# Adding each expert's rows to the tokens' rows in DRAM by accumulating indirect DMAs

## The chip, the core and the metric

The kernel runs on one core of a Trainium2 chip. The metric is device time in microseconds (us), the median of several executions. A profiled execution is taken beside them; its trace is what this text reads. The engines are named as the trace names them: PE is TensorE (matmul), PEld its weight loads, DVE is VectorE, ACT is ScalarE, POOL is GpSimd, SP is SyncE, which here only issues DMAs. A q behind a name (SPq) is that engine's instruction sequencer.

## What is computed

Two blocks run one after the other on 512 tokens of 1024 numbers. The first (`first_block`: recurrent and sparse attention layers) isn't touched by the change. The second has two layers; each mixes tokens (attention, convolution, memory) and then sends every token through two of 16 experts:

```python
def grouped_moe(x2d, w_router, router_bias, w_gate, w_up, w_down):
    logits = (x2d @ w_router).astype(jnp.float32) + router_bias.astype(jnp.float32)
    scores = jax.nn.softmax(logits, axis=-1)
    grouped = scores.reshape(T, N_GROUPS, EXPERTS_PER_GROUP)
    g_idx = jnp.argmax(jnp.max(grouped, axis=-1), axis=-1)
    in_group = jnp.take_along_axis(grouped, g_idx[:, None, None], axis=1)[:, 0]
    top_vals, top_idx = lax.top_k(in_group, TOP_K)
    experts = g_idx[:, None] * EXPERTS_PER_GROUP + top_idx
    weights = top_vals / jnp.sum(top_vals, axis=-1, keepdims=True)
    ...
        h = jax.nn.silu(xblk @ w_gate[e]) * (xblk @ w_up[e])
        return h @ w_down[e]
    ...
    return jax.ops.segment_sum(y, buf_tok, num_segments=T + 1)[:T]
```

The layer's end is `x = layer_norm(DEEPNORM_ALPHA * x + f, ln2_g[l], ln2_b[l])` with `f` from the function above. Gate and up weights of an expert are 1024 by 512, the down weights 512 by 1024, all fp32: 2 MB each, 6.29 million bytes an expert. With 512 tokens and two choices each there are 1024 rows for 16 experts, 64 on average. With these inputs every expert of the first layer has between 43 and 90 tokens; in the second layer they have between 22 and 142, and expert 15 alone has more than 128.

## The kernel before

Each matmul of an fp32 activation with an fp32 weight is done as three matmuls of rounded parts (high by high, high by low, low by high; `mm3`, L183 to L185). A weight tile (512 KB) is loaded on SP's queue by `wload` (L1622, tiles `wr` and `mr`, up to nine of them in buffers), and `wsplit` makes its high part on ScalarE (L1636) and its low part on VectorE (L1637).

`moe` (L1758) runs one layer's experts in order. Each expert has 128 slots, filled from slot 0 by the rank of a token among those that chose the expert. The rows of experts 0 and 1 are picked by matmuls with one-hot matrices (`expert_in`). For experts 2 to 14, `slot_tokens` (L1683) works out on VectorE and TensorE which token sits in which slot (`idx`, L1712; a free slot gets an index past the last token), and `expert_fetch` (L1715) gathers the tokens' rows from the DRAM copy `x1d` by an indirect DMA on POOL (L1718), three experts ahead; `expert_turn` transposes them on TensorE (L1729). `expert_up` does gate and up, `expert_down` (L1749) the down product of the expert before. Its two halves are copied out of PSUM by ScalarE (L1755, tile `yo`) and written to the expert's 128 slots in DRAM, `yd`, by two DMAs of 256 KB on ScalarE's queue (L1756).

Before expert 2, a loop (L1769 to L1783) runs once for every block of 128 rows by which experts overflow their slots: not at all in the first layer, once in the second. It loads that expert's weights again, and writes its rows to further slots of `yd`. So that slots never written hold numbers, `clear_slots` (L1481) writes 8 blocks of zeros (512 KB each) to `yd` early in the kernel, some 1400 us before they are used.

`x1d` holds the layer's normalised tokens. `after_mix` (L1398) and `late_copy` (L1433) write it, with `put` (L538): two SP DMAs of 256 KB for each of four tiles of 128 tokens.

At a layer's end `weigh` (L1592) gives each token's two weights (done beside expert 2), and the four token tiles are loaded back from `x1d` in eight SP DMAs of 256 KB, issued in program order at expert 14. Expert 15 keeps its rows on chip. The rows of experts 0 to 14 come back from `yd` by eight indirect gathers on POOL (`yg`, L1829, 512 KB each: four token tiles, two choices), and are added with their weights on VectorE (`add`, L1838; ten instructions a layer) and, for some, by fp32 matmuls with diagonal matrices on TensorE (L1846; `dg` made on POOL, L1821). Expert 15's rows are added by matmuls with its one-hot matrix (L1848, `ct`) and an addition from PSUM (L1849). `combine(0, ..)` makes tiles 0 and 1 ready, whose layer norm follows (L1313 to L1327); `combine(2, ..)` does tiles 2 and 3 and is ordered behind the statistics of the first two (`stats_end`). The work on the tail is ordered by hand: `issue_after` keeps an instruction behind a named one.

A tile's `tag` and `bufs` set how many buffers it shares; the scheduler places waits where a buffer, a PSUM bank or a DRAM tensor is written again or read after a write.

Of the kernel before, what the change touches and what calls it, by code (L numbers as in the profile page):

```python
# [33 lines left out]
ON_PE = [(2, 0), (3, 0)]  # L34
RAW = 5, 2
ORDER = (0, 2, 1, 2, 0, 2, 2, 1, 2, 0, 2, 1)
SLOTS = (16 + N_OV) * P
# [3 lines left out]
T2 = (26, 29, 45, 21)  # L41
# [6 lines left out]
class K:  # L48
# [515 lines left out]
    def hawk(self, x, after, prep, masks, rest):  # L564
# [833 lines left out]
    def after_mix(self, l, xs, i0, gb, pl, sc, x1):  # L1398
# [27 lines left out]
        if late:  # L1426
            self.parted = self.split_end[0]
        else:
            for a in range(2):
                self.affine(xs[a], xs[a], gb, nc.gpsimd, nc.gpsimd)  # L1430
                self.put(self.x1d[l], a, xs[a])

    def late_copy(self, l, xs, gb):  # L1433

        for i in range(2, 4):
            with self.tc.issue_after(self.routed.ins):
                self.affine(xs[i], xs[i], gb, self.nc.vector, self.nc.gpsimd)
            self.put(self.x1d[l], i, xs[i])

    def moe_constants(self):  # L1440
# [37 lines left out]
        self.yd = self.dp.tile([SLOTS, D], F32, name="yd")  # L1478
        self.x1d = [self.dp.tile([T, D], F32, name=f"x1d{l}") for l in range(2)]

    def clear_slots(self):  # L1481

        nc = self.nc
        z = self.rt("zero")
        nc.gpsimd.memset(z, 0.0)
        blocks = [self.yd[i * P:(i + 1) * P] for i in range(15, 16 + N_OV)]
        self.later += [lambda d=d: nc.sync.dma_start(d.rearrange("p (h c) -> p h c", h=2),
                                                      z[:, None, :].to_broadcast([P, 2, 512])) for d in blocks]
# [103 lines left out]
    def weigh(self, oh1, oh2, sc, slotf):  # L1592
# [10 lines left out]
        wl, w1 = [self.small([4], name=f"rwl{j}", bufs=1) for j in range(2)]  # L1603
        tt(wl, oh1[:, :, 15], wv[:, 0], op=OP.mult)
        tt(w1, oh2[:, :, 15], wv[:, 1], op=OP.mult)
        tt(wl, wl, w1, op=OP.add)
        slot = self.small([4, 2], I32, name="rslot", bufs=1)
        nc.vector.tensor_copy(slot.rearrange("p i j -> p j i"), slotf)
        return slot, wv, wl
# [73 lines left out]
    def slot_tokens(self, ohs, rank):  # L1683
# [4 lines left out]

        tok = self.small([2, 4, 16], name="tok", bufs=1)
        for u in range(2):  # L1690
            nc.gpsimd.iota(tok[:, u], pattern=[[u * P, 4], [0, 16]], base=0, channel_multiplier=1 - u,
                           allow_small_or_imprecise_dtypes=True)
# [3 lines left out]
        tk = self.small([2, 4, 2, 16], BF16, name="stk", bufs=1)  # L1696
        at = self.ph.tile([P, 2, 4, P], BF16, name="at", tag="t2", bufs=self.bufs["t2"])
        for j, oh in enumerate(ohs):
            tt(a, oh, rank, op=OP.mult)
            nc.vector.tensor_reduce(r[:, j], a, axis=AX.X, op=OP.add)  # L1700
            for u in range(2):
                tt(tk[:, j, :, u], oh, tok[:, u], op=OP.mult)
            for i in range(4):
                nc.vector.tensor_scalar(at[:, j, i], self.iota, r[:, j, i:i + 1], None, op0=OP.is_equal)
        for j in range(2):
            for i in range(4):
                nc.tensor.matmul(ps[:, :32], at[:, j, i], tk[:, j, i].rearrange("p u e -> p (u e)"),
                                 start=j == 0 and i == 0, stop=j == 1 and i == 3)
        idx = self.small([16], I32, name="idx", bufs=1)
        hi = self.small([16], name="idh", bufs=1)  # L1710
        nc.vector.tensor_copy(hi, ps[:, 16:32])
        tt(idx, ps[:, :16], hi, op=OP.add)  # L1712
        return idx
# [35 lines left out]
    def expert_down(self, hT, wd, yrow, own=False):  # L1749
        nc = self.nc  # L1750
        for c in range(2):
            py = self.pj()
            self.tm(self.wrows(wd[:, c * 512:(c + 1) * 512], 4, own), hT, py)
            yo = self.t2(F32, "yo")
            nc.scalar.copy(yo, py)  # L1755
            nc.scalar.dma_start(yrow[:, c * 512:(c + 1) * 512], yo)  # L1756

    def moe(self, l, xs, rt):  # L1758
# [10 lines left out]
        def overflow():  # L1769
            nov = nc.values_load(ovi[0:1, 7:8], min_val=0, max_val=N_OV)  # L1770
            with tc.For_i(0, nov, 1) as b:
                ev = nc.values_load(ovi[0:1, bass.ds(b, 1)], engines=[mybir.EngineType.SP], min_val=0, max_val=15)
                row = b * P + 16 * P
                we = [w[bass.ds(ev, 1)].rearrange("o k c -> (o k) c") for w in W]
                oh = self.f4(F32R, "oh").rearrange("p (i a s) -> p i a s", i=4, a=2)
                for i in range(4):
                    nc.vector.tensor_scalar(oh[:, i, 1], cur, slotf[:, 0, i:i + 1], None, op0=OP.is_equal)
                    nc.vector.scalar_tensor_tensor(oh[:, i, 0], cur, slotf[:, 1, i:i + 1], oh[:, i, 1].bitcast(F32),
                                                   op0=OP.is_equal, op1=OP.add)
# [3 lines left out]
                self.expert_down(hT, we[2], self.yd[bass.ds(row, P)], True)  # L1783

        xT = [[[v[:, a * P:(a + 1) * P] for v in t] for t in xT] for xT in [self.expert_in(l, xs, oh, 256)] for a in range(2)]
        idx = self.slot_tokens((oh1, oh2), rank)
        fetched = {e: self.expert_fetch(l, idx, e) for e in (2, 3)}
        hT = None
        for e in range(16):
# [8 lines left out]
            if e == 15:  # L1798
                self.expert_down(hT, W[2][14], self.yd[14 * P:15 * P])
            h2 = self.expert_up(xT[e], *[self.wrows(W[j][e], 8, first=first.pop(0) if first else None) for j in range(2)])  # L1800
            if e == 2:
                slot, wv, wl = self.weigh(oh1, oh2, sc, slotf)
            if e == 14:
                f = [self.load_x(self.x1d[l], i) for i in range(4)]
            if 0 < e < 15:
                self.expert_down(hT, W[2][e - 1], self.yd[(e - 1) * P:e * P])
# [7 lines left out]
        pw = self.pt()  # L1814
        for i in range(4):
            nc.tensor.matmul(pw[:, :1], oh[:, i].bitcast(F32), wl[:, i:i + 1], start=i == 0, stop=i == 3)
        dg = self.t2(F32, "dg")
        for i in range(2):
            for j in range(2):
                k = 2 * i + j  # L1820
                nc.gpsimd.tensor_scalar(dg[:, k * P:(k + 1) * P], self.ident, wv[:, j, i + 2:i + 3], None, op0=OP.mult)  # L1821
        ws = self.small([1], name="ws", bufs=1)
        nc.vector.tensor_copy(ws, pw[:, :1])
        raws = [self.wload(W[2][15][:, c * 512:(c + 1) * 512], 4) for c in range(2)]
        gs = []
        for i in range(4):
            for j in range(2):
                g = self.eh.tile([P, D], F32, name="yg", tag="mr", bufs=RAW[0]) if j else self.f4(F32, "yg")
                nc.gpsimd.indirect_dma_start(out=g, out_offset=None, in_=self.yd,  # L1829
                                             in_offset=bass.IndirectOffsetOnAxis(ap=slot[:, i, j:j + 1], axis=0))  # L1830
                gs.append(g)
        half = [slice(h * 512, (h + 1) * 512) for h in range(2)]

        def add(i, j):
            for h in range(2):
                if (i, h) in ON_PE:
                    continue
                nc.vector.scalar_tensor_tensor(f[i][h], gs[2 * i + j][:, half[h]], wv[:, j, i:i + 1], f[i][h],  # L1838
                                               op0=OP.mult, op1=OP.add)

        def combine(p, h):
            for i in range(p, p + 2):
                ps = self.pj()
                for j in range(2) if (i, h) in ON_PE else (1,) if p else ():
                    k = 2 * i + j - 4
                    nc.tensor.matmul(ps, dg[:, k * P:(k + 1) * P], gs[2 * i + j][:, half[h]], start=j == 0 or (i, h) not in ON_PE, stop=False)  # L1846
                for part in range(2):
                    nc.tensor.matmul(ps, ct[:, i * P:(i + 1) * P], y[h][part], start=not p and part == 0, stop=part == 1)  # L1848
# [3 lines left out]
        mark = self.split_end[0]  # L1852
        for c in range(2):
            py = self.pj()
            ws2 = list(self.wsplit(raws[c]))
            if c:
                with tc.issue_after(mark.ins):
                    for i in range(2):
                        for j in range(2):
                            add(i, j)  # L1860
            for k, wk in enumerate(ws2):
# [4 lines left out]
            last = nc.scalar.activation(h, py, AF.Identity, bias=0.0, scale=ws)  # L1866
            self.lo(lo, py, h, ws)
# [4 lines left out]
        for i in range(2, 4):  # L1872
            with tc.issue_after(mark.ins):
                add(i, 0)
        with tc.issue_after(self.stats_end.ins):
            for h in range(2):
                combine(2, h)
# [26 lines left out]
def body(tc, I, out, stop=None):  # L1904
    with ExitStack() as es:
# [55 lines left out]
        if stop and stop.endswith("1"):  # L1961
            src = I["hawk_out"][0]
            with k.phase("pre", t2=34, e=(2,), r=8):
# [6 lines left out]
                if stop == "first1":  # L1970
                    k.clear_slots()
# [76 lines left out]
```

## Time and profile before

| | before |
|---|---|
| median of 3 runs | 2987.15 us (2984.01 to 2990.06) |
| profiled execution | 2984.6 us, span of the trace 2982.8 us |
| granted TensorE clock over the span | 0.979 of full |
| experts, first layer | about 1615 to 1950 us |
| experts, second layer | about 2595 to 2960 us |

The span runs from the first to the last recorded instruction. The chain of waits goes back from the last instruction, at each step to what released it. In the timeline a row is an instruction or a run of equal ones: start, duration, engine and line, what is written from what, and in brackets how long the engine was idle before it and what it waited for. Durations of matmuls overlap, since they are pipelined. The windows show each engine's busy time in a stretch, the granted clock of TensorE (1.00 is full speed), the mean busy share of 16 DMA engines, and the rate at which they moved data.

### The profile page before, as it was taken

What the parts mean: (1) busy time and instruction counts of PE and PEld (TensorE: products, weight loads), DVE (VectorE), ACT (ScalarE), POOL (GpSimd) and SP (SyncE); (2) the same over time, 40 slices, a digit from 0 to 9 for tenths busy, and PEclk for the clock granted to TensorE, in tenths of its full rate; (3) what the DMA queues carried; (4) which work ended last, traced back from release to release, by engine and by line L of the source; (5) the groups of instructions that cost most, each with busy time, mean ns of one, the idle gap of its engine ahead of it and who ended that gap; (6) DMA issues with size and microseconds to landing.
All of it is one profiled execution on the core that took longest, in us unless ns stands there. A gap on an engine that the chain in (4) does not pass through costs nothing. (4 is left out here: it accounts for less than half of the span.)

```text
span 2982.8 us, 42706 instructions
## 1 busy us (share of the span) xinstructions
PE 2836.1 (95%) x15979; PEld 2373.0 (80%) x15979; DVE 1940.5 (65%) x3869; ACT 1548.4 (52%) x2725; POOL 166.0 (6%) x190
## 2 busy tenths in 40 slices
PE   8999999999999999999997999969999999889995
PEld 6888878876669999878797787759987878767873
DVE  4454567566656677343467788888755344878987
ACT  4343477456655455222444788735443243468883
POOL 0000000000000000000011100140000000210002
PEclk9999999999999999999998999989999999899997
DMA  4242324431016312323264999932222334479996
GB/s 136 86 146 86 106 85 148 142 102 43 26 33 219 100 58 65 91 92 92 90 203 159 346 392 393 373 126 64 65 71 89 95 108 147 149 261 393 392 391 226
DMA packets 344235, 476.48 MB, mean 160 GB/s; under 512 B 25334, under 2 KB 209368, under 8 KB 344024
## 3 DMA queue, kind: packets, MB, share of 16 engines
q1 hardware_dynamic: 325464, 430.18, 42.9%
q0 software_dynamic: 6336, 23.07, 2.0%
q10 hardware_dynamic: 12224, 20.46, 1.9%
q8 instruction: 127, 2.08, 0.3%
q14 instruction: 84, 0.69, 0.1%
HBM read 440.56 MB, written 33.08 MB: 159 GB/s over the span
## 5 line engine op out<-in xcount | busy, mean ns | idle before, releaser
L163 DVE TENSOR_TENSOR wl<-wr,wh 128x1024 fp32r<-128x1024 f32 x348 | 421.8, 1214 | 440.7 <-ACT wh L162 436.5
L162 ACT CAST wh<-wr 128x1024 fp32r<-128x1024 f32 x352 | 363.1, 1032 | 566.3 <-PE pj L184 336.9
L183 PE MATMUL pj<-x,wh 128*128 128x512 f32 x1288 | 508.2, 395 | 0.6 <-ACT x L109 0.6
L184 PE MATMUL pj<-x,wh 128*128 128x512 f32 x1288 | 507.8, 394 | 0.0
L185 PE MATMUL pj<-x,wl 128*128 128x512 f32 x1288 | 506.1, 393 | 0.4 <-DVE wl L163 0.4
L185 PEld LDWEIGHTS pj<-x,wl 128*128 128x128 f32 x1288 | 242.0, 188 | 54.4 <-issue 4.7
L183 PEld LDWEIGHTS pj<-x,wh 128*128 128x128 f32 x1288 | 242.0, 188 | 52.5 <-issue 4.6
L184 PEld LDWEIGHTS pj<-x,wh 128*128 128x128 f32 x1288 | 242.0, 188 | 52.1 <-issue 5.6
L210 PE MATMUL pj<-wh,x 128*128 128x256 f32 x864 | 248.7, 288 | 3.8 <-DVE xb L276 3.1
L211 PE MATMUL pj<-wl,x 128*128 128x256 f32 x864 | 246.9, 286 | 0.0
L212 PE MATMUL pj<-wh,x 128*128 128x256 f32 x864 | 245.1, 284 | 0.0
L210 PE MATMUL pj<-wh,yh 128*128 128x256 f32 x640 | 180.9, 283 | 0.4 <-ACT wh L162 0.2
L211 PE MATMUL pj<-wl,yh 128*128 128x256 f32 x640 | 178.9, 280 | 1.3 <-DVE wl L163 1.3
L212 PE MATMUL pj<-wh,yl 128*128 128x256 f32 x640 | 178.7, 280 | 0.4 <-DVE yl L126 0.3
L210 PEld LDWEIGHTS pj<-wh,x 128*128 128x128 f32 x864 | 166.0, 192 | 5.2 <-DVE xb L276 3.5
L211 PEld LDWEIGHTS pj<-wl,x 128*128 128x128 f32 x864 | 166.2, 192 | 0.4
L212 PEld LDWEIGHTS pj<-wh,x 128*128 128x128 f32 x864 | 166.1, 192 | 0.3
L1637 DVE TENSOR_TENSOR ml<-mr,mh 128x1024 fp32r<-128x1024 f32 x108 | 132.0, 1222 | 28.4 <-ACT mh L1636 28.1
L1637 DVE TENSOR_TENSOR wl<-mr,wh 128x1024 fp32r<-128x1024 f32 x106 | 129.5, 1222 | 29.2 <-ACT wh L1636 21.7
L1636 ACT CAST mh<-mr 128x1024 fp32r<-128x1024 f32 x108 | 113.2, 1048 | 29.2 <-PE pj L185 10.6
L211 PEld LDWEIGHTS pj<-wl,yh 128*128 128x128 f32 x640 | 120.9, 189 | 2.4 <-DVE wl L163 2.1
L1636 ACT CAST wh<-mr 128x1024 fp32r<-128x1024 f32 x106 | 111.1, 1049 | 21.7 <-DMA mr<-in_w_exp_down 6.5
(513 smaller groups left out, 6320.6 us busy)
## 6 DMA issues: line engine op xcount, KB each, us to landing
wr<-in_w_in SPq DMA_DIRECT2D x124, 512.0 KB, 3.7
mr<-in_w_exp_gate SPq DMA_DIRECT2D x76, 512.0 KB, 8.3
mr<-in_w_exp_up SPq DMA_DIRECT2D x72, 512.0 KB, 7.5
mr<-in_w_exp_down SPq DMA_DIRECT2D x66, 512.0 KB, 9.0
wr<-in_w_exp_down SPq DMA_DIRECT2D x62, 512.0 KB, 9.1
wr<-in_hawk_w_in SPq DMA_DIRECT2D x60, 512.0 KB, 3.6
wr<-in_w_exp_up SPq DMA_DIRECT2D x56, 512.0 KB, 7.9
wr<-in_w_exp_gate SPq DMA_DIRECT2D x52, 512.0 KB, 7.5
```

The lines of the kernel that those rows point to most:

```text
L162: self.nc.scalar.copy(wh[:, :kt, :c], raw[:, :kt, :c])
L163: eng.tensor_tensor(wl[:, :kt, :c], raw[:, :kt, :c], wh[:, :kt, :c].bitcast(F32), op=OP.subtract)
L183: mm(ps, a[0], b[0], start=first, stop=False)
L184: mm(ps, a[0], b[1], start=False, stop=False)
L185: mm(ps, a[1], b[0], start=False, stop=last)
L210: mm(d, tok(x[k][0]), w[k][0][:, :n], start=k == 0 and a == 0, stop=False, skip_group_check=True)
L211: mm(d, tok(x[k][0]), w[k][1][:, :n], start=False, stop=False, skip_group_check=True)
L212: mm(d, tok(x[k][1]), w[k][0][:, :n], start=False, stop=end, skip_group_check=True)
L1636: self.nc.scalar.copy(wh, raw)
L1637: self.nc.vector.tensor_tensor(wl, raw, wh.bitcast(F32), op=OP.subtract)
```

## The change

The slots in DRAM go. A second DRAM copy of the tokens, `acc`, one for each layer, is written beside `x1d`. `expert_down` now multiplies each row by its slot's weight as ScalarE copies it out of PSUM, into a tile `yo` of 128 by 1024, and one indirect DMA on POOL adds the 128 rows to the tokens' rows in `acc`. Rows of free slots get an index of at least 512 and are left out by the bounds check. `slot_tokens` also works out each slot's weight and whether it is filled (48 columns in place of 32, in fp32), so `weigh` runs ahead of it. The loop's rows get their lists by eight small matmuls. At the end `f` is loaded from `acc` in four SP DMAs of 512 KB, behind the last accumulation, and `combine` adds expert 15's rows alone. `combine(2, 0)` moves ahead, between expert 15's down matmuls.

```diff
-T2 = (26, 29, 45, 21)
+T2 = (26, 29, 45, 17)
...
-            self.clear_slots()
...
-                self.put(self.x1d[l], a, xs[a])
+                for d in (self.x1d[l], self.acc[l]):
+                    self.put(d, a, xs[a])
...
-            self.put(self.x1d[l], i, xs[i])
+            for d in (self.x1d[l], self.acc[l]):
+                self.put(d, i, xs[i])
...
+    def slot_lists(self, ps, n):
...
+        nc.vector.tensor_copy(idx, ps[:, :n])
+        nc.vector.tensor_copy(w, ps[:, n:2 * n])
+        nc.vector.tensor_scalar(free, ps[:, 2 * n:3 * n], -2.0 * T, 2.0 * T, op0=OP.mult, op1=OP.add)
+        nc.vector.tensor_tensor(add, ps[:, :n], free, op=OP.add)
+        return idx, add, w
...
-    def expert_down(self, hT, wd, yrow, own=False):
-        nc = self.nc
+    def expert_down(self, hT, wd, l, add, w, own=False):
+
+        nc = self.nc
+        yo = self.ph.tile([P, D], F32, name="yo", tag="yo", bufs=2)
         for c in range(2):
             py = self.pj()
             self.tm(self.wrows(wd[:, c * 512:(c + 1) * 512], 4, own), hT, py)
-            yo = self.t2(F32, "yo")
-            nc.scalar.copy(yo, py)
-            nc.scalar.dma_start(yrow[:, c * 512:(c + 1) * 512], yo)
+            nc.scalar.activation(yo[:, c * 512:(c + 1) * 512], py, AF.Identity, bias=0.0, scale=w)
+        nc.gpsimd.indirect_dma_start(out=self.acc[l], out_offset=bass.IndirectOffsetOnAxis(ap=add, axis=0), in_=yo,
+                                     in_offset=None, bounds_check=T - 1, oob_is_err=False, compute_op=OP.add)
...
-        idx = self.slot_tokens((oh1, oh2), rank)
+        idx, add, ws, each = self.slot_tokens((oh1, oh2), rank, self.weigh(oh2, sc))
+        down = lambda e, hT: self.expert_down(hT, W[2][e], l, add[:, e:e + 1], ws[:, e:e + 1])
...
-            if e == 14:
-                f = [self.load_x(self.x1d[l], i) for i in range(4)]
...
+        raws = [self.wload(W[2][15][:, c * 512:(c + 1) * 512], 4) for c in range(2)]
+        f = []
         for i in range(4):
-            nc.tensor.matmul(pw[:, :1], oh[:, i].bitcast(F32), wl[:, i:i + 1], start=i == 0, stop=i == 3)
...
+            t = self.f4(F32, "f")
+            nc.sync.dma_start(t, self.acc[l][i * P:(i + 1) * P])
+            f.append([t[:, :512], t[:, 512:]])
...
-                for j in range(2) if (i, h) in ON_PE else (1,) if p else ():
-                    k = 2 * i + j - 4
-                    nc.tensor.matmul(ps, dg[:, k * P:(k + 1) * P], gs[2 * i + j][:, half[h]], start=j == 0 or (i, h) not in ON_PE, stop=False)
...
-                if c == 1 and k == 1:
-                    combine(0, 0)
+                if c == 1 and k in (1, 2):
+                    combine(2 * k - 2, 0)
...
         with tc.issue_after(self.stats_end.ins):
-            for h in range(2):
-                combine(2, h)
+            combine(2, 1)
```

## Rows read from the trace of the kernel before

**Rows 1.** the page: span, and busy time of TensorE and VectorE

```profile
span 2982.8 us, 42706 instructions
...
PE 2836.1 (95%) x15979; PEld 2373.0 (80%) x15979; DVE 1940.5 (65%) x3869; ACT 1548.4 (52%) x2725; POOL 166.0 (6%) x190
```

**Rows 2.** windows: start:end, length, busy PE PEld DVE ACT POOL, PEclk, DMA share, GB/s

```profile
1739.20:1757.40 18.20, 18.20 (x85) 14.66 (x84) 15.79 (x16) 14.65 (x18) 0.94 (x1) 1.00 1.05 392
1849.30:1867.90 18.60, 18.55 (x85) 14.56 (x84) 16.52 (x17) 15.26 (x18) 0.94 (x1) 1.00 1.05 393
...
2911.00:2923.00 12.00, 9.83 (x35) 7.08 (x33) 5.35 (x5) 6.21 (x9) 0.00 (x0) 0.86 1.04 386
```

**Rows 3.** queues (packets, MB, share of 16 engines), then issues (us to landing)

```profile
q0 software_dynamic: 6336, 23.07, 2.0%
q10 hardware_dynamic: 12224, 20.46, 1.9%
...
yd<-yo ACTq DMA_DIRECT2D x62, 256.0 KB, 5.8
...
xg<-x1d,idx POOLq DMA_INDIRECT x28, 7.2
```

**Rows 4.** chain of the late second layer, then TensorE's timeline there

```profile
2901.11 8.80 DMA x<-x1d
...
2909.97 6.02 DMA mr<-in_w_exp_down
...
2917.17 0.50 PE L183 MATMUL pj<-mh,hh 128*128 128x512 f32 x1 [1.41 <-ACT mh L1636]
2918.43 0.79 PE L184 MATMUL pj<-ml,hh 128*128 128x512 f32 x1 [0.76 <-DVE ml L1637]
```

**Rows 5.** chain of the second layer's end

```profile
2935.02 0.80 PE pt L1816 x8
...
2936.12 6.08 DMA yg<-yd,rslot
...
2947.93 3.75 PE pj L1846 x4
...
2952.15 1.29 DVE x L1849 x2
...
2955.47 0.62 DVE x L1838
...
2958.53 2.39 DVE x L1849 x4
```

**Rows 6.** chain of the first layer's end

```profile
1927.20 6.65 DMA yg<-yd,rslot
...
1944.58 2.17 DVE x L1838
...
1946.86 2.64 DVE x L1838
...
1951.95 2.39 DVE x L1849 x4
```

**Rows 7.** TensorE's timeline at the overflow loop's exit in each layer, ScalarE's before it

```profile
1662.90 0.69 PE L1729 MATMUL pt<-ident,xg 128*128 128x128 f32 x2 [2.91 <-SPq L1771]
...
2669.72 0.69 PE L1729 MATMUL pt<-ident,xg 128*128 128x128 f32 x2 [3.86 <-issue]
...
2666.52 0.35 ACTq L1756 DMA_DIRECT2D yd<-yo  x1
```

**Rows 8.** timelines of POOL and TensorE at the first layer's first fetched expert

```profile
1632.85 2.43 POOL L1718 DMA_INDIRECT xg<-x1d,idx  x1 [38.50 <-DVE idx L1712]
...
1642.38 0.69 PE L1729 MATMUL pt<-ident,xg 128*128 128x128 f32 x2 [3.50 <-DMA xg<-x1d,idx]
```

**Rows 9.** ScalarE's copies of expert rows, and its scaled ones (min/median/max ns)

```profile
L1755 ACT COPY yo<-pj x62: 572/587/595, 1657.2 to 2921.5; 128x512 f32<-128x512 f32 x62
...
L1866 ACT ACTIVATE ylh<-pj,ws x4: 687/688/688, 1933.8 to 2945.9; 128x512 fp32r<-128x512 f32 x4
```

More of the change, by code (lines that the diff above doesn't have):

```diff
@@ L1477, in moe_constants @@
                     nc.vector.tensor_tensor(s, s, rb, op=OP.add)
-        self.yd = self.dp.tile([SLOTS, D], F32, name="yd")
+        self.acc = [self.dp.tile([T, D], F32, name=f"acc{l}") for l in range(2)]
         self.x1d = [self.dp.tile([T, D], F32, name=f"x1d{l}") for l in range(2)]
-    def clear_slots(self):
-        nc = self.nc
[L1484 to L1488, printed above, removed]
     def first_max(self, v, oh, t, mx):
@@ L1590, in places, with weigh @@
         return oh1, oh2, sc, slotf, rank, ovi, oh01
-    def weigh(self, oh1, oh2, sc, slotf):
+    def weigh(self, oh2, sc):
         nc = self.nc
@@ L1602, in weigh @@
         tt(wv[:, 1], wv[:, 1], wv[:, 0], op=OP.mult)
[L1603 to L1609, printed above, removed]
+        return wv
     def wload(self, ap, kt, own=False):
@@ L1681, in expert_slots, with slot_tokens @@
         return oh.rearrange("p i a s -> p i (a s)")
-    def slot_tokens(self, ohs, rank):
+    def slot_tokens(self, ohs, rank, wv):
         nc = self.nc
         tt = nc.vector.tensor_tensor
[L1689 to L1692, printed above, removed]
+        tok = self.small([4, 16], name="tok", bufs=1)
+        nc.gpsimd.iota(tok, pattern=[[P, 4], [0, 16]], base=0, channel_multiplier=1, allow_small_or_imprecise_dtypes=True)
+        one = self.small([2, 4, 3], name="tkv", bufs=1)
+        nc.gpsimd.memset(one, 1.0)
         ps = self.pt()
@@ L1695, in slot_tokens @@
         r = self.small([2, 4], name="str", bufs=1)
[L1696 to L1697 removed]
+        tk = self.t2(F32, "tk")[:, :384].rearrange("p (j i u e) -> p j i u e", j=2, i=4, u=3)
         for j, oh in enumerate(ohs):
+            at = self.t2(F32, "at").rearrange("p (i s) -> p i s", i=4)
             tt(a, oh, rank, op=OP.mult)
             nc.vector.tensor_reduce(r[:, j], a, axis=AX.X, op=OP.add)
[L1701 to L1702 removed]
+            tt(tk[:, j, :, 0], oh, tok, op=OP.mult)
+            tt(tk[:, j, :, 1], oh, wv[:, j, :, None].to_broadcast([P, 4, 16]), op=OP.mult)
+            nc.vector.tensor_copy(tk[:, j, :, 2], oh)
+            nc.gpsimd.tensor_copy(one[:, j, :, 0], tok[:, :, 0])
+            nc.gpsimd.tensor_copy(one[:, j, :, 1], wv[:, j])
             for i in range(4):
[L1704 to L1705 removed]
+                nc.vector.tensor_scalar(at[:, i], self.iota, r[:, j, i:i + 1], None, op0=OP.is_equal)
             for i in range(4):
[L1707 removed]
+                nc.tensor.matmul(ps[:, :48], at[:, i], tk[:, j, i].rearrange("p u e -> p (u e)"),
                                  start=j == 0 and i == 0, stop=j == 1 and i == 3)
[L1709 to L1713, printed above, removed]
+        return self.slot_lists(ps, 16) + (one,)
+    def slot_lists(self, ps, n):
+        nc = self.nc
+        idx, add = [self.small([n], I32, name=f"{k}{n}", bufs=1) for k in ("idx", "ida")]
+        w, free = [self.small([n], name=f"{k}{n}", bufs=1) for k in ("wsl", "idf")]
+        nc.vector.tensor_copy(idx, ps[:, :n])
[3 more added lines that the diff above has]
+        return idx, add, w
     def expert_fetch(self, l, idx, e):
@@ L1776, in overflow @@
                 for i in range(4):
-                    nc.vector.tensor_scalar(oh[:, i, 1], cur, slotf[:, 0, i:i + 1], None, op0=OP.is_equal)
-                    nc.vector.scalar_tensor_tensor(oh[:, i, 0], cur, slotf[:, 1, i:i + 1], oh[:, i, 1].bitcast(F32),
-                                                   op0=OP.is_equal, op1=OP.add)
+                    for j in range(2):
+                        nc.vector.tensor_scalar(oh[:, i, 1 - j], cur, slotf[:, j, i:i + 1], None, op0=OP.is_equal)
+                pw = self.pt()
+                for i in range(4):
+                    for j in range(2):
+                        nc.tensor.matmul(pw[:, :3], oh[:, i, 1 - j].bitcast(F32), each[:, j, i], start=i == 0 and j == 0,
+                                         stop=i == 3 and j == 1)
+                _, ad, wo = self.slot_lists(pw, 1)
+                nc.vector.tensor_tensor(oh[:, :, 0], oh[:, :, 0].bitcast(F32), oh[:, :, 1].bitcast(F32), op=OP.add)
                 nc.vector.tensor_scalar(cur, cur, float(P), None, op0=OP.add)
@@ L1798, in moe @@
             if e == 15:
-                self.expert_down(hT, W[2][14], self.yd[14 * P:15 * P])
+                down(14, hT)
             h2 = self.expert_up(xT[e], *[self.wrows(W[j][e], 8, first=first.pop(0) if first else None) for j in range(2)])
-            if e == 2:
-                slot, wv, wl = self.weigh(oh1, oh2, sc, slotf)
-            if e == 14:
-                f = [self.load_x(self.x1d[l], i) for i in range(4)]
             if 0 < e < 15:
-                self.expert_down(hT, W[2][e - 1], self.yd[(e - 1) * P:e * P])
+                down(e - 1, hT)
             hT = h2
@@ L1843, in combine @@
                 ps = self.pj()
-                for j in range(2) if (i, h) in ON_PE else (1,) if p else ():
-                    k = 2 * i + j - 4
-                    nc.tensor.matmul(ps, dg[:, k * P:(k + 1) * P], gs[2 * i + j][:, half[h]], start=j == 0 or (i, h) not in ON_PE, stop=False)
                 for part in range(2):
-                    nc.tensor.matmul(ps, ct[:, i * P:(i + 1) * P], y[h][part], start=not p and part == 0, stop=part == 1)
+                    nc.tensor.matmul(ps, ct[:, i * P:(i + 1) * P], y[h][part], start=part == 0, stop=part == 1)
                 nc.vector.tensor_tensor(f[i][h], f[i][h], ps, op=OP.add)
         y = []
-        mark = self.split_end[0]
         for c in range(2):
             py = self.pj()
[L1855 to L1861, printed above, removed]
+            for k, wk in enumerate(list(self.wsplit(raws[c]))):
                 self.mm3(py, hT[k], wk, k == 0, k == 3)
-                if c == 1 and k == 1:
-                    combine(0, 0)
+                if c == 1 and k in (1, 2):
+                    combine(2 * k - 2, 0)
             h, lo = self.t2(F32R, "ylh"), self.t2(F32R, "yll")
-            last = nc.scalar.activation(h, py, AF.Identity, bias=0.0, scale=ws)
-            self.lo(lo, py, h, ws)
+            last = nc.scalar.activation(h, py, AF.Identity, bias=0.0, scale=ws[:, 15:16])
+            self.lo(lo, py, h, ws[:, 15:16])
             y.append((h, lo))
@@ L1969, in body @@
                 k.rope_tables()
-                if stop == "first1":
-                    k.clear_slots()
                 for i in range(0, 4, 2):
```

31 lines of the change are left out of this document (1 added, 30 removed).

## The prediction

> **What bounds the kernel now.** I read the page first, then the windows, then the chain of waits near the end of each expert layer. The page says that TensorE is busy 95% of a span of 2982.8 us [rows 1]; what matters is which stage still has waits. The windows of one expert each are to be read with two columns side by side. In an early one of the first layer TensorE is busy for all of its 18.20 us, while the DMA engines are full too, at 392 GB/s; in a later one an expert takes 18.60 us and TensorE's wait has begun [rows 2]. So TensorE's floor is 18.2 us an expert, and the DMA engines stand beside it: weights (6.29 MB), the gathered rows (0.52 MB) and the slots written (0.52 MB) are 7.34 MB, which at 393 GB/s takes 18.7 us. That is 0.48 us over the floor, 6.2 us over 13 experts; only about five late experts show 0.4 us each, 2 us in all, so weights loaded ahead cover the other 4.2 us. VectorE (16 to 17 us) and ScalarE (15 us) have room. Any DMA time that the change adds or takes in this stage therefore matters, once those 4.2 us are used up.
>
> The chain then shows two places that are not steady. Near the layer's end the reload of the tokens, `x<-x1d`, stands ahead of the last weights on SP's queue: 8.80 us, then 6.02 us for a weight tile, and TensorE idles 1.41 and 0.76 us [rows 4]. The window behind it has a granted clock of 0.86 over 12 us [rows 2], which costs 12 x 0.14 = 1.7 us more: 3.9 us together. And the tail waits for the gathers (6.08 us in the second layer, 6.65 in the first), then runs additions and fp32 matmuls that nothing covers [rows 5, 6].
>
> **Part by part.**
>
> *The tail of the second layer.* The fp32 weight matmuls (0.80 us) stand on the chain, then the fp32 diagonal matmuls (3.75 us), then two additions of `yg` (0.62 each, 1.24); all go. Of the four last additions from PSUM (2.39 us) two move ahead between the down matmuls, 1.2 us [rows 5]. Sum: 7.0 us less. The gathers' wait lies beside the down matmuls and I don't count it again.
>
> *The tail of the first layer.* Here the diagonal matmuls are covered by VectorE's additions. The two `yg` additions of 2.17 and 2.64 us go, and half of 2.39 us as above [rows 6]. These two are slow, over three times the 0.62 us of the second layer [rows 5], so whatever slows VectorE then will slow what takes their place; I count half of 4.81 us. Sum: 3.6 us less (between 2.4 and 6).
>
> *The reload.* It moves behind expert 15's last weights on SP's queue, which it passes with four DMAs of 512 KB in place of eight. The stall of 3.9 us goes in the second layer, and I take as much in the first, where the same rows repeat: 7.8 us less. What hides the new loads: expert 14's rows leave ScalarE at about 2922 [rows 9]; an accumulation that lands 8 us later (one issue and the 7.2 us of a gather [rows 3]) and 2.1 MB at 393 GB/s (5.3 us) put `f` there by about 2936, while the gathered rows in whose place it stands came at 2942.2 (2936.12 + 6.08 [rows 5]). If that cover is gone, each us late is a us of the end.
>
> *The loop.* TensorE can't pass the loop's exit before transfers in flight have landed: it idled 2.91 us in the first layer, on SP, and 3.86 us in the second, after a write issued at 2666.52 [rows 7]. The accumulation is issued after both halves instead of one half at a time, has POOL's issue ahead of it, and an indirect DMA lands 7.2 us after its issue against 5.8 us for a write [rows 3]. In the first layer the accumulation of expert 0 stands ahead of the loop, with its second half (0.6 us [rows 9]) and 1.4 us more of landing and up to 2 us of POOL: +4 us (from -1, if it is issued behind the loop, to +5). In the second layer the loop's own accumulation: +2.5 us (0 to +5). What is queued behind the wait on SP and TensorE is the weights and transposes of the next experts.
>
> *The lists.* `weigh` (six small VectorE instructions) stands ahead of the first index now, and the sum of two index parts goes. In the first layer TensorE waits 3.50 us for the first fetched rows, issued on POOL at 1632.85 [rows 8], so a delay there would show: 0, between -2 and +2 us a layer.
>
> *Edits at nothing.* The scaled copy takes 688 ns in place of 587 [rows 9], 0.2 us an expert on ScalarE, which has 3 us free and loses two DMA issues of 0.35 us [rows 7]. The extra puts (2.1 MB a layer) and the zero writes that go lie in stretches where the DMA engines are not full; at worst 5 us a layer, if the puts delay the first weights. The loop's eight small matmuls and its lists are under 2 us.
>
> *The accumulation itself.* This is the unknown. The trace has no accumulating DMA, so I bound the time s that it takes of the busiest DMA engine by the nearest rows. The gathers: 2.0% of the span for 44 of them (23.07 MB of 0.52 MB each) is 59.7 / 44 = 1.36 us each. The writes it replaces: 1.9%, of which 16.25 of 20.46 MB are `yd`, over 31 experts' rows, 1.45 us each [rows 3]. A steady expert then needs 18.7 - 1.45 + s of DMA time. Low end: only filled rows move, 64 on average, evenly over the engines, s = 0.68. High end: each filled row costs two passes, since its destination must be read too, and the rows, which fill an expert's slots from the front, lie on half of the engines: 64 rows on half are 1.36 us, twice is s = 2.7. In between lie 1.36 (one pass on half of the engines, or two passes spread evenly) and 2.04 (one and a half). I take s = 1.36, nearest to both rows, so that the steady stage stays as it is: 0.
>
> The rows bear the gathers out as 6336 / 44 = 144 packets each, one for a row of 4 KB and some for the end [rows 3], so what is moved goes by row. [...]
>
> **Sum.** -7.0 - 3.6 - 7.8 + 4 + 2.5 = -11.9 us. From the profiled execution's 2984.6 us that is 2972.7 us; it stood 2.55 us under the median of 2987.15, and the median is what I predict: 2975 us.
>
> **Rivals.** A, a light accumulation (s = 0.68): a steady expert needs 17.9 us of DMA, under the floor, and the 2 us of stalls in each layer go too: 2971 us. For it: half the rows are empty.
>
> B, the forecast: 2975 us, with a range of its own of 2969 to 2983 from the loop's and the lists' ends.
>
> C, a middling accumulation (s = 2.04): a need of 19.3 us, 1.07 over the floor; 13 x 1.07 - 4.2 = 9.7 us of waits in place of 2. Against that the reload's full 5.3 us count in place of 3.9. +6.3 us a layer, 12.6 in all: 2988 us, no change. The point at which the gain is used up is s = 2.0.
>
> D, the slower side: two passes on half of the engines (s = 2.7). Need 19.95 us, 13 x 1.75 - 4.2 = 18.6 us of waits; +15 us a layer, 30 in all: 3006 us. It is slower by more than can be told from no change once s is over 2.25 us. For it speaks that an addition must read what it adds to, and that the DMA engines are full in just this stage [rows 2]. Against it: a spread of rows over the engines that doesn't go by slot.
>
> W, the accumulation is light but lands late: the loop's exits at their upper ends (+3.5 us) and `f` some 5 us late at each tail: 2988 us. This is also the case in which the change doesn't do what it says at the end: it would turn the wait for gathers into one for accumulations.
>
> **How the numbers follow.** Chances: A 0.10, B 0.38, C 0.28, D 0.18, W 0.06. A measurement of this kernel can tell about 0.2%, 6 us, from no change, so faster is under 2981. Faster: A, 0.34 of B and 0.02 of C, 0.46. Within: 0.04 of B, 0.20 of C, 0.04 of W, 0.28. Slower: 0.06 of C, D and 0.02 of W, 0.26. The range from 2969 to 3007 leaves out half of D above, and the lowest of A and B below. B's own is given above.
>
> **What would show it.** Right: in windows of one expert 18.2 to 18.6 us with no growing TensorE idle time; at the layer's end no `x<-x1d` in the chain and a granted clock of 1.00; in the tail no wait for `f`. Wrong: late windows of 19 us or more with TensorE waiting for weights (C, D), the accumulations' share of the engines over 2 us each; TensorE idle at the loop's exit by 8 us or more; a chain that ends in `f<-acc` (W); POOL held by an accumulation while a fetch stands behind it, which would show as TensorE waiting for `xg`.

## The result

The change made the kernel slower: 3003.97 us, median of six runs (2998.55 to 3007.14), against 2986.63 us for the kernel before, a ratio of 1.0057 with a 95% interval of 1.0046 to 1.0068. That is 17 us more where 12 us less were forecast. It lies inside the range that was given (to 3007 us), beside rival D at 3006 us. The profiled execution took 3007.14 us, 3 us over the median.

The page of the changed kernel, first its span and busy times, then POOL's DMA queue (packets, MB, share of 16 engines) and two kinds of issue (count, median us from issue to landing):

```profile
span 3005.4 us, 42673 instructions
...
PE 2834.7 (94%) x15971; PEld 2371.5 (79%) x15971; DVE 1928.3 (64%) x3852; ACT 1550.3 (52%) x2727; POOL 214.0 (7%) x204
...
q0 software_dynamic: 8496, 22.28, 2.6%
...
acc<-yo,ida POOLq DMA_INDIRECT x31, 8.8
xg<-x1d,idx POOLq DMA_INDIRECT x28, 7.7
```

TensorE's busy time is the one of before [rows 1], within 2 us; so the 22.6 us by which this span is longer are waits. The queue's share tells more. It moves less than before (22.28 MB against 23.07 [rows 3]) and takes more, 2.6% of the span, 78.1 us. The 28 fetches at 1.36 us are 38.1 us of it; 40.0 us are left for 31 accumulations, 1.29 us each as a mean of 16 engines, for only half as many rows as a gather moves.

Windows of the changed kernel, with the columns of [rows 2]: an early and a late expert of the first layer, a late one of the second, then the stretch in which expert 15's last weights arrive.

```profile
1693.70:1711.80 18.10, 18.10 (x85) 14.65 (x84) 15.64 (x16) 13.84 (x17) 4.05 (x2) 1.00 1.03 369
1865.20:1885.30 20.10, 19.00 (x86) 14.37 (x85) 16.66 (x17) 15.07 (x19) 4.12 (x2) 1.00 1.01 355
2863.20:2883.00 19.80, 18.85 (x86) 14.41 (x85) 16.71 (x17) 15.12 (x19) 4.12 (x2) 1.00 1.04 375
...
2951.80:2961.80 10.00, 8.82 (x41) 6.30 (x39) 6.93 (x7) 6.25 (x7) 1.56 (x1) 1.00 0.60 201
```

Early experts still run at TensorE's floor (busy 18.10 of 18.10 us). Late ones take 19.8 to 20.1 us against 18.6 [rows 2]. The DMA engines are as busy as before (share 1.0) and move less: 355 to 375 GB/s against 393. The last window is the one to look at twice: 40% of the DMA time is idle, and yet the chain shows TensorE's last weights on their way for 13.21 us:

```profile
2949.09 13.21 DMA wr<-in_w_exp_down
...
2962.32 1.05 ACT wh L1621
```

A load that takes so long beside idle engines fits some engines that are late and others that have nothing to do. The trace's records of single packets show as much: from 2952 to 2955 us 16 to 17 packets of the weight loads are under way at once, in the mean of each us, and from 2957 to 2962 us 0.7 to 2.0. The trace doesn't name the engines, so that these are the ones with the added rows is an argument here; the first experiment tests it. No load of `f` stands on the chain at either layer's end, so rival W doesn't show.

At the loop's exits TensorE idles 8.73 us in the first layer and 7.07 us in the second, against 2.91 and 3.86 [rows 7]:

```profile
1672.82 0.69 PE L1723 MATMUL pt<-ident,xg 128*128 128x128 f32 x2 [8.73 <-issue]
...
2692.35 0.69 PE L1723 MATMUL pt<-ident,xg 128*128 128x128 f32 x2 [7.07 <-issue]
```

### The profile page after: what moved, and what is told of

The parts are those of the page before. It is cut to its first block, busy times and chain, and to the rows that moved or that the text cites. A ratio compares the mean times of both kernels' runs of the same rounds, so it can differ in the third digit from the quotient of the medians.

```text
span 3005.4 us, 42673 instructions
## 1 busy us (share of the span) xinstructions
PE 2834.7 (94%) x15971; PEld 2371.5 (79%) x15971; DVE 1928.3 (64%) x3852; ACT 1550.3 (52%) x2727; POOL 214.0 (7%) x204
## 3 DMA queue, kind: packets, MB, share of 16 engines
q0 software_dynamic: 8496, 22.28, 2.6%
## 4 chain that ended last, share of the span: by engine, by line
PE 71%; DVE 11%; DMA 9%; ACT 5%; issue 3%; SPq 0%; POOL 0%; POOLq 0%; ACTq 0%; DVEq 0%
PE pj L182 13%; PE pj L183 13%; PE pj L181 13%; PE pj L209 5%; PE pj L208 5%; PE pj L210 5%; DMA wr<-in_w_exp_down 4%; DMA mr<-in_w_exp_down 3%; PE ps L444 2%; PE po L1014 2%; PE ps L445 2%; DVE wl L161 1%; PE pt L1025 1%; PE po L1201 1%; PE pt L252 1%
```

## The experiments

Ratios are to the kernel before, run beside it on the same chip, with 95% intervals; a difference of 0.001 is 3 us. Where stretches of two kernels are compared, it is by when the same matmul starts in each trace. Packet records are the trace's rows for single pieces of a DMA; here one row of 4 KB is one packet.

**Slots spread over both halves** (one line of the changed kernel):

```diff
-        nc.gpsimd.iota(self.iota, pattern=[[1, P]], base=1, ...)
+        nc.gpsimd.iota(self.iota, pattern=[[1, 2], [2, 64]], base=1, ...)
```

> One change to the changed kernel: the list of slot numbers is 1, 3, 5, .. for partitions 0 to 63 and 2, 4, 6, .. for 64 to 127, so that an expert's filled slots lie on both halves of the partitions; the same rows are added. Theory E (the addition takes the DMA engines' time: a filled row costs two passes, 0.327 us in the trace against 0.16 for a gathered one, and the filled rows sit on half of the engines, 8 rows or 2.6 us on the busiest for 64 rows): the busiest engine has 4 rows, 1.3 us, a steady expert goes from 19.2 us on average back to about 18.4, the two layers win 10 to 14 us, 2990 to 2994 us. At most 9 rows of 64 are under way at once in the trace now; it should be 13 to 16. Rival L (the accumulations cost by their latency, on POOL or at the loop's exit, or by their bytes, which do not change): the time stays within 3 us of 3004.

Measured: 2984.45 us, ratio 0.9998 (0.9983 to 1.0012). The whole loss is gone, 0.0059 or 17.6 us, with the same rows, bytes and issues. That is more than expected: in the traces the steady experts get back about 11 us, inside the 10 to 14, and the tails 7.6 us more. Late experts of the two layers, and the stretch at the last weights:

```profile
1857.00:1875.90 18.90, 18.65 (x86) 14.38 (x85) 16.47 (x16) 15.03 (x19) 4.12 (x2) 1.00 1.03 367
2846.60:2865.50 18.90, 18.63 (x86) 14.39 (x85) 16.47 (x16) 15.03 (x19) 4.12 (x2) 1.00 1.05 380
2933.20:2943.20 10.00, 8.98 (x42) 6.75 (x41) 8.27 (x9) 6.84 (x9) 1.60 (x1) 1.00 0.76 250
```

and its accumulations:

```profile
q0 software_dynamic: 8496, 22.28, 2.7%
...
acc<-yo,ida POOLq DMA_INDIRECT x31, 7.7
```

They take as much engine time as in the changed kernel (2.7% against 2.6%), but land in 7.7 us instead of 8.8. In the packet records the rows of one accumulation that are under way at the same moment are 7 to 11 in the changed kernel and 10 to 19 here (last four of the first layer, 48 to 69 rows each). So how many engines share an accumulation goes by the slots of its rows: 7 to 11 rows at once, of 16 engines, are about half. That is read from these counts, as the trace names no engine; "half of the engines" below stands for it. By the 17.6 us it was the busier half that set the time. The late loads bear it out: where the changed kernel's chain waits 12.56 and 13.21 us for the last weights of the two layers, the chain of this kernel has no DMA over the same stretches. Rival L falls: the bytes and the issues are the same, and the gathers, whose slots are in a new order too, land in 7.7 us in both kernels. The landing of an accumulation did get 1.1 us shorter; what such waits are worth by themselves is seen in the second layer below. The time, 2984.45 us, lies under the 2990 to 2994 us that were expected.

**Plain writes in place of additions, and no accumulations at all.** Two kernels, the first with `compute_op=OP.add` left out, the second without the DMA.

> The changed kernel with the addition left out of the scatter: the same rows are written over the tokens' rows, not added to them, so the sums are missing from the result. Theory E: a filled row costs one pass, 0.16 us, so 1.3 us on the busiest engine for 64 rows: like the spread rows, 2990 to 2994 us, steady experts at 18.2 to 18.6 us. Rival L: rows, POOL's issues and waits are as before, so 3004 us within 3. Rival H (only the placing on half of the engines costs, not the addition): no change in a row's time of 0.327 us, 3004 us.

> The changed kernel without its 31 accumulating DMAs; the experts' rows are made and weighted, but never reach the tokens (all but expert 15's are missing from the result). It prices all that the accumulations cost, with their waits. Theory E: steady experts at TensorE's floor, 18.2 us, about 12 us less; the loop's exits wait for no accumulation, 6 to 9 us less; so 2980 to 2987 us; what is then left over the forecast of 2975 lies outside the accumulations. Rival L: the steady stage stays at over 19 us an expert, and only the exits go: 2995 us.

Measured: 2952.63 us (ratio 0.9883, 0.986 to 0.9905) and 2974.09 us (0.9963, 0.995 to 0.9975). Neither total can be read: without the sums the second layer gets other inputs and routes otherwise, and in the first of the two its loop ran no times. What can be read is the first layer. Between the matmuls that the kernel before runs at 1687 and 1868 us (its steady experts) it loses 9.6 us on that kernel in the changed one, 3.2 us in the spread one, 3.4 us with plain writes and 2.2 us without any. Plain writes on half of the engines (3.4 us) cost as little as additions spread over both halves (3.2 us). A filled row's packet takes 0.159 us with plain writes and 0.327 us with the addition, in the changed and in the spread kernel alike; rival H, that only the placing costs, falls. In the kernel without accumulations late experts still don't come down to the floor:

```profile
1833.10:1852.00 18.90, 18.64 (x85) 14.39 (x84) 16.48 (x16) 14.91 (x19) 1.76 (x1) 1.00 1.01 359
```

They take 18.87 us, with TensorE waiting 0.26 us for VectorE's low part once an expert, while the DMA engines move 359 GB/s. So a second, smaller cost has nothing to do with accumulations; two runs below look at it.

**The same in the second layer alone**, which keeps the routing:

```diff
-                                     in_offset=None, bounds_check=T - 1, oob_is_err=False, compute_op=OP.add)
+                                     in_offset=None, bounds_check=T - 1, oob_is_err=False, **({} if l else dict(compute_op=OP.add)))
```

and, in the other kernel, `if l: return` ahead of it.

> The changed kernel with the addition left out in the second layer alone: there the rows are written over the tokens' rows, so the output lacks the second layer's sums, while the first layer, and with it the routing of the second, are as in the changed kernel (in the run without any additions the second layer's routing was another, and its loop ran no times, so its time couldn't be compared). Theory E: a row's time falls from 0.327 to 0.16 us, and the second layer wins what spreading the slots won there, about 9 us: 2994 to 2996 us. If only the placing cost: 3004 us.

> The changed kernel without accumulating DMAs in the second layer alone (their rows are missing from the output; the routing is kept). Theory E: beyond the 9 us of the run before, only the loop's exit and the last wait win, some 4 to 5 us: 2989 to 2992 us. If accumulations cost mainly by what waits for their landing, this run wins much more over the plain writes than those win over the additions.

Measured: 2996.58 us, ratio 1.0029 (1.0017 to 1.0042), and 2992.2 us, 1.0015 (1.0006 to 1.0025). Adding in place of writing (0.327 against 0.159 us a row, theory E's second pass) is worth 0.0028, 8.4 us, in one layer; taking the writes away as well gives 4.2 us more, of which the loop's exit and the last wait are to be paid. The first interval lies clear of the changed kernel's; the second overlaps the first's, so the 4.2 us are not clear of noise. As gains over the changed kernel, 8.4 and 12.5 us, both are what theory E expected; the times themselves are 0.6 and 0.2 us above the ranges. The steady stage says it more sharply. Between the matmuls that the kernel before runs at 2715 and 2893 us the changed kernel loses 6.2 us, the spread one 1.6, the one with plain writes 1.6 and the one without any 1.8, with the same routing in all four. So what accumulations cost there is the second pass on half of the engines (6.2 against 1.6 us), and what is left is not theirs. About 2 of the 4.2 us lie at the loop's exit, where TensorE idles 4.85 us with plain writes and 2.68 without. The queue's share shows the halving:

```profile
q0 software_dynamic: 8496, 22.28, 2.3%
```

2.3% of 2994.4 us is 68.9 us; less 38.1 for the fetches and 15 additions at 1.29 us, 11.4 us are left for 16 plain writes, 0.71 us each against 1.29.

**The zero writes put back**

```diff
             self.moe_constants()
+            self.clear_slots()
             self.rope_tables()
```

> The changed kernel with the eight zero writes of 512 KB put back on SP's queue, to a tensor that nothing reads. In the trace TensorE falls behind by some 4 us at 170 to 178 us, where the loads and small tables that stood behind those writes now run earlier, ahead of weight splits. Theory Z (the removed writes held the small tables back): that stretch is as before, 3 to 5 us less, 2999 to 3001 us. Rival V (that shift is from run to run): within 2 us of 3004, and the other kernels show the shift or not by chance.

Measured: 3006.66 us, 1.0061 (1.0041 to 1.0081): no gain in the whole that could be told. The stretch itself, from 170 to 180 us, in the kernel before:

```profile
170.00:180.00 10.00, 9.47 (x62) 7.98 (x61) 9.53 (x32) 8.01 (x14) 0.33 (x1) 1.00 0.75 274
```

in the changed kernel:

```profile
170.00:180.00 10.00, 7.32 (x47) 6.58 (x46) 9.65 (x34) 8.64 (x14) 0.40 (x1) 0.84 0.25 62
```

and with the zero writes:

```profile
170.00:180.00 10.00, 9.48 (x67) 8.44 (x66) 9.53 (x31) 8.14 (x14) 1.11 (x1) 1.00 0.85 279
```

Without them TensorE is busy 7.3 of 10 us and its granted clock falls to 0.84. All kernels of this study agree: at 184 us the nine without the zero writes are 2.9 to 6.5 us behind the trace of before, the four others that have them -0.3 to 2.1, a difference of 3.6 us in the mean. So this part is shown for its stretch. It doesn't last: at 1585 us, ahead of the expert layers, the nine are 2.0 to 8.8 us behind the trace of before and the four 4.1 to 6.7, 5.2 and 5.3 us in the mean. The kernels drift apart by some us in between whatever they hold, so nothing here shows that the zero writes are worth anything in the whole, and the total is inconclusive. That the small tables and loads ahead of the weight splits are the way in which it works was only read from the order in the trace, not tried by itself.

**The order of the transposes written out**, in the changed kernel and in the spread one:

```diff
-                xT.append(self.expert_turn(fetched.pop(e + 1)))
+                xT.append(self.expert_turn(fetched.pop(e + 1), self.mm_end if e > 2 else None))
...
+                with self.tc.issue_after(end.ins) if end else nullcontext():
                     self.nc.tensor.transpose(...)
```

> The changed kernel with one order written out: the transposes of the next expert's rows stay behind the last matmul of the down product, as in the kernel before. In the changed kernel, from about the eighth expert of a layer on, four of the eight stand ahead of the last five matmuls; those experts take 18.87 us even where no accumulation runs, against 18.37 before. Theory S (this order costs 0.5 us an expert, 12 experts, wherever the DMA engines don't cost more): here the late experts wait for weights anyway (19.6 us), so only 0 to 3 us less, 3001 to 3004 us. If the order were the whole cause of the loss: 12 us less or more.

> The kernel with the slots spread over both halves, and the order of the transposes written out. Theory S with theory E: the late experts fall from 18.87 to 18.4 us, 12 of them, so 6 us under the 2984.5 us of the spread kernel: 2978 to 2979 us. Rival: the weights are late by then (need 17.2 + 1.3 = 18.5 us of DMA time), and the experts stay at 18.6 to 18.9 us: 2982 to 2985 us.

Measured: 3005.1 us, 1.0048 (1.0031 to 1.0064), and 2985.82 us, 0.9987 (0.9978 to 0.9997). In the changed kernel the order gives nothing that can be told from it, as expected: a late expert takes 19.9 us with it. In the spread one the ratio falls by 0.0011, 3 us, with intervals that overlap, so the total doesn't decide. The trace does: a late expert goes from 18.87 to 18.65 us (the window holds 18.70), in some ten experts, and the last step of each layer is 0.3 us shorter, 3 us in all. Such experts take about 18.87 us in every kernel of this study that has the new order and doesn't wait for weights, and about 18.64 us in the three, this one and the two below, that combine spread slots with the order written out:

```profile
1838.80:1857.50 18.70, 18.62 (x86) 14.45 (x85) 16.54 (x17) 15.08 (x18) 3.41 (x2) 1.00 1.04 379
```

That is half of what theory S asked for. TensorE is busy 18.62 of 18.70 us; the rest of the way to 18.4 is in small waits between matmuls of which I didn't find the cause.

**The reload alone, in the kernel before**

```diff
-            if e == 14:
-                f = [self.load_x(self.x1d[l], i) for i in range(4)]
...
+        f = [self.load_x(self.x1d[l], i) for i in range(4)]
         gs = []
```

> The kernel before with one part of the change alone: the reload of the tokens' rows stands behind expert 15's last weights on SP's queue in place of ahead of expert 14's. The prediction's step: the stall of 3.9 us in each layer goes, 7.8 us less than 2985 us, 2977 us. Rival: the tail then waits for the reload beside the gathers (2.1 MB more among 4.2 MB), and gives half of it or more back: 2981 to 2985 us.

Measured: 2983.86 us, 0.9987 (0.9978 to 0.9997), 4 us less: the rival's half. The stall is gone: at its place (1905 to 1915 us and 2915 to 2925 us of the kernel before) this run wins 4.0 and 4.3 us. The chain shows where half of it went:

```profile
2928.21 6.01 DMA mr<-in_w_exp_down
...
2940.48 9.87 DMA yg<-yd,rslot
```

The gathers' wait grows from 6.08 us [rows 5] to 9.87 us, with the reload now among them.

**Expert 0's accumulation behind the loop**, on the spread kernel with the order written out:

```diff
                 overflow()
+                held()
...
-                down(e - 1, hT)
+                held = down(e - 1, hT)
+                if e > 1:
+                    held()
```

> The kernel with slots spread and the order written out, and expert 0's accumulation issued behind the overflow loop in place of ahead of it. Theory X (the loop's exit waits for transfers under way to land, and this one is the last): TensorE's wait at the first layer's exit falls from 10 us to about 6, which is what it was without any accumulation, 4 us less in that layer; in the second layer the loop's own accumulation is the last, so nothing there: 4 us under the run with the same order, 2974 to 2975 us. Rival: the exit waits for the fetches or the weights anyway: within 1.5 us of it.

Measured: 2983.92 us, 0.9982 (0.997 to 0.9995), against 0.9987: the intervals overlap, so the total doesn't decide. The exit does. With the order alone:

```profile
1670.54 0.69 PE L1724 MATMUL pt<-ident,xg 128*128 128x128 f32 x2 [8.89 <-issue]
```

and with the accumulation behind the loop:

```profile
1666.17 0.69 PE L1724 MATMUL pt<-ident,xg 128*128 128x128 f32 x2 [4.70 <-ACT wh L1621]
```

4.2 us less at the place where 4 were expected, and the same as in the first layer of the kernel without accumulations (4.71 us).

**All together, and the measures that need no change.** The first kernel has the spread slots, the order, the accumulation behind the loop, the zero writes, and gathers that leave out free slots' rows:

```diff
-                    fetched[e + 3] = self.expert_fetch(l, idx, e + 3)
+                    fetched[e + 3] = self.expert_fetch(l, add, e + 3, False)
```

> Slots spread, order written out, expert 0's accumulation behind the loop, and two parts more: gathers from expert 4 on leave out the rows of free slots (the same bounds check as the accumulation's), and the eight zero writes stand on SP's queue again. DMA need of a steady expert: 6.29 MB of weights and half of 0.52 MB, 16.7 us, and 1.3 us of accumulation: 18.0 us, under TensorE's floor of 18.2. Theory E: no waits for weights in any steady expert; with the 18.63 us of the written order, and 3 to 4 us less at the start: 0.994 to 0.997 of the kernel before. Rival: the late experts are held by VectorE's order, not by weights, so the gathers bring nothing: 0.997 to 0.999.

The second is the kernel before with the reload behind the weights and the same gathers.

> The kernel before, with the reload behind the last weights and with gathers that leave out free slots' rows from expert 4 on; no accumulation. What the same two measures are worth without the change: need 18.0 + 0.7 - 0.7, about 18.0 us, so the 0.2 to 0.4 us of late waits go, 3 to 4 us over both layers beyond the 4 us of the reload: 0.997 to 0.998 of the kernel before.

Measured: 2974.37 us, 0.9956 (0.9942 to 0.9971), and 2985.39 us, 0.9992 (0.9983 to 1.0001). The first beats both kernels, by 13 us the one before and by 30 us the changed one. One of its late experts:

```profile
1834.40:1853.10 18.70, 18.61 (x86) 14.46 (x85) 16.53 (x17) 14.88 (x18) 3.41 (x2) 1.00 1.01 354
```

Late experts take 18.63 us in both layers, as without the shorter gathers, though these moved 6.1 MB less (16.16 MB on POOL's queue). So weights no longer bind there, and the gathers alone bring little in this stage; the 0.0026 over the run before, whose interval just touches this one's, are the zero writes and the gathers together, not told apart. Without the accumulation the same gathers bring nothing that the totals tell, 0.9992 against the reload's 0.9987, and 3 to 4 us were expected: a miss.

## Why the prediction was wrong, step by step

*The accumulation itself is the step that failed.* It set s, the time on the busiest DMA engine, to 1.36 us, "nearest to both rows", and so the steady stage's term to 0. It is 40.0 us / 31 = 1.29 us as a mean over 16 engines, and if the rows lie on half of them, as the counts of the spread run say (7 to 11 rows at once against 10 to 19), about twice that on the busier half: by this estimate 2.6 us (64 rows on 8 engines, 8 of 0.327 us each), the high end that was given (2.7). The steady stages lost 9.6 and 6.2 us in place of 0. Both halves of that end were needed, and each was tried by itself: one pass on half of the engines (plain writes), or two passes on all of them (spread), costs about what the old writes did (3.4 and 3.2 us more in the first layer's steady stage, 1.6 each in the second's). Rival D had the two premises and, by this estimate, the s right, at a chance of 0.18; its total was right partly by luck, as its place was only half right (below). The argument from "the nearest row" was the fault: both rows are of transfers that add nothing and fill all 128 partitions, so neither bore on the two questions that decided.

No run had shown either premise of the high end, the second pass or the half of the engines, when the sum was made. The runs showed since 0.327 against 0.159 us a row, a factor of 2.06, and 17.6 us from the placing alone.

*Where D's price lay.* D put nearly all of its 30 us over the forecast into the steady stage. There the changed kernel loses 9.6 us in the first layer and 6.2 in the second. The rest came at the tail, where D had nothing: the last weights come late (12.56 and 13.21 us on the chain), and the two tails win 2.9 and 7.3 us where 7.5 and 10.9 were forecast. D's 3006 us came so near because it had too much in the one place and nothing in the other.

*The tails and the reload, right.* With the rows spread, from a matmul late in the layer to the next layer's first products or the end, the first layer wins 6.8 us (forecast 3.6 + 3.9) and the second 11.0 (7.0 + 3.9). At the reload's place itself it wins 3.9 and 4.3 us, and so does the changed kernel, so that term was right in both layers. That it is kept to the end needs the gathers to be gone too; alone it gives half, as the reload run shows. So those two terms belong to one another, which the sum did not say.

*The loop, right in kind and too small.* Forecast +4 and +2.5 us; the exits' idle time grew by 5.8 and 3.2 us. The deferred accumulation takes 4.2 us of it back in the first layer.

*The lists.* Forecast 0, between -2 and +2 us a layer. TensorE's wait of 3.50 us for the first fetched rows [rows 8] is gone, and from expert 0's first products to just ahead of the loop's exit the changed kernel wins 2.3 us in the first layer (the spread one 2.4); in the second it loses 2.0 (1.5) in the stretch that ends there, the loop's own lists included. So 0 is about right as a sum, from two ends and not from nothing happening.

*Edits at nothing.* The zero writes were set at nothing for a stretch with room on the DMA engines. Without them the kernel falls 3.6 us behind at 170 to 180 us, but the distance is gone ahead of the expert layers, so no run shows a cost of theirs in the whole. One cost had no step at all: the scheduler placed half of the next transposes ahead of the last down matmuls, 3 us by the spread traces. The spread kernel, with its engines evened out, is still some 11 us over 2975 (0.9998 of 2986.63). By its trace it loses 3.2 and 1.6 us in the steady stages, part of that by the transposes' order, and its exits' idle time grew 2.8 us more than forecast: nearly 8 of the 11. The rest is open; two runs of one kernel differ by more.

One sentence ahead of the prediction is wrong: in the kernel before, a free slot's fetch index is 0, not one past the last token, so its gathers move all 128 rows, as 23.07 MB / 44 shows. The sum used the 0.52 MB and isn't touched by it.

## What to carry to other kernels

Before a DMA that adds is put where the DMA engines are full, count its rows twice (here 0.327 us each against 0.159 for a plain write), and ask how many engines they keep at work: here rows that fill the first partitions were 7 to 11 at once, against 10 to 19 with the slots spread, and a weight load beside them took 13.21 us. Spread partly filled lists over the partitions; here that was one line and 17 us. When the trace shows no transfer of the kind that a change adds, take the bound that a reason speaks for, not the row that is nearest in name.

## What was not expected of the hardware

A row of 4 KB took 0.327 us when it was added in DRAM, and 0.159 us when it was written. A row left out by the bounds check still had a packet, of 8 bytes, which took 0.009 us, so leaving rows out was nearly free. Behind a mean DMA share of 0.60 a load of 512 KB took 13.21 us, with 0.7 to 2.0 of the weight loads' packets under way at once in its last 5 us, and with the rows spread that wait was gone: here the mean hid what was late. And taking eight DMAs of 512 KB away from a queue with room (DMA share 0.75) made the stretch 3.6 us longer in the mean, with TensorE busy 7.3 of 10 us in place of 9.5 and the granted clock at 0.84 in place of 1.00. That this is because what stood behind them came forward was not tried.
